# Every fourth weight tile split by the DMA: a casting load for the high part, a negation and an accumulating load for the low part

## The chip, the cores and the metric

The kernel runs on one core of one Trainium2 chip. The metric is the device time of one execution in microseconds (us). A core has a matrix engine (PE; its weight loads are listed apart as PEld), a vector engine (DVE), a scalar engine (ACT), a general-purpose engine (POOL), a queue engine that here only issues loads and stores (SP), and 16 DMA engines that all queues share.

## The reference

One layer of a streaming encoder over 256 frames of 2048 features, all in float32:

```python
xn = rmsnorm(h, norm_mix_w)
q, k, v, r, glr, gu, gv, gates = split(xn @ w_in)        # w_in: 2048 x 14352
o_gla = gla_branch(q, k, v, glr, r, ...)                 # gated linear attention
o_gmlp = gmlp_branch(gu, gv, ...)                        # spatial gating in blocks of 128 frames
g = sigmoid(gates + b_gate)
h = h + sum_b(g[b] * (branch[b] @ w_branch[b])) @ w_out  # 2 x 2048 x 2048, 2048 x 2048
hn = rmsnorm(h, norm_mlp_w)
h = h + square(relu(hn @ w_ff_up)) @ w_ff_down           # 2048 x 8192, 8192 x 2048
y = rmsnorm(h, norm_final_w)
```

Nearly all of the arithmetic is the six weight products; about 306 MB of weights are read once.

## The kernel before

**Precision.** PE multiplies in a reduced float32 format (`F32R`). To keep float32 accuracy every operand is held as two such tiles, a high part (the value rounded to `F32R`) and a low part (the value minus its high part). A product is three matmuls: high by high (L197), low activation by high weight (L198) and high activation by low weight (L199).

**Tiling.** `gemm` (L185) makes 256 tokens by 512 output columns from 2048 features. It goes over the features in 8 steps; each step needs one weight tile of 256 rows by 512 columns (512 KB; on chip 128 partitions by 1024 elements) and runs 2 feature blocks x 2 token tiles x 3 = 12 matmuls on it. A whole execution has 576 weight tiles. The matmuls of all products stand in one fixed order on PE.

**Preparing a weight tile.** `split_weights` (L170 to L183) does it in three steps on three engines. SP loads the tile into a buffer `w` (L178). ACT copies it into `wh`, which rounds it: the high part (L179). DVE subtracts `wh` from `w` into `wl`: the low part (L180). There are 5 buffers for `w` and 4 each for `wh` and `wl`, given out in turn. So the tile numbered i uses the `wh` and `wl` buffers of tile i-4, and its high part can be written only when the last matmul that reads the high part of tile i-4 (an L198) is done.

**What sets the order.** A scheduler arranges the instructions of ACT, DVE, POOL and the queues by its own estimate; each engine then runs its list in order, and waits on semaphores. During the first product (`in_order`) ACT and DVE keep the written order. Short steps (transposes, attention, norms) wait in `pending` and are worked off between weight tiles by `drain`.

**POOL** issues no DMA before. It has some memsets and, in `rsqrt_of` (L306), 20 small powers of one or two columns for the norms. ACT also moves finished products out of PSUM (`scaled`, L326), for example.

Of the kernel before, what the change touches and what calls it, by code (L numbers as in the profile page):

```python
# [9 lines left out]
F32 = mybir.dt.float32  # L10
# [32 lines left out]
class Operand:  # L43
    """An activation with features on partitions, as high and low parts: tiles of 4 K-tiles."""

# [10 lines left out]
def block_kernel(  # L56
# [21 lines left out]
    nc = tc.nc  # L78
# [18 lines left out]
    def pair_tile():  # L97
        """[128, 2, 512]: 512 features of both token tiles, tokens on partitions"""
        return slots.tile([P, NTT, CB], F32, tag="slot", name=uid("pair"))
# [18 lines left out]

    # As long as `in_order` is set, the steps on the way to the products keep their order.
    in_order = [True]  # L120

    def pin(ins):
        return tc.keep_in_program_order(ins) if in_order[0] else ins

    # Steps that need TensorE for a short time wait here, and run between the K-tiles of the
    # next large product, when what they read is long there.
    pending = deque()
# [4 lines left out]

    # ---- x, in blocks of 256 features; constants
    h = cpool.tile([P, NTT, D], F32, name="h")
# [6 lines left out]
    def late(dst, src):  # L141
        """A load that must not run ahead of the weights'."""
        tc.keep_in_program_order(nc.scalar.dma_start(dst, src))
# [15 lines left out]
    def to_partitions(src, n, name):  # L159
        """[n, 128] -> [128, n]"""  # L160
        dst = cpool.tile([P, n], F32, name=name)
        tp = tr_ps()
        nc.tensor.transpose(tp[:, 0:n], src, ident[0:n, 0:n])
        pin(nc.vector.tensor_copy(dst, tp[:, 0:n]))
        return lambda i: dst[:, i : i + 1]

    mix_col = to_partitions(vec_n, KT, "mixw")

    # ---- shared steps
    def split_weights(src, by_k=False):  # L170
        """[128, nk, n] of DRAM -> its high and low parts in SBUF."""
        k, n = src.shape[1], src.shape[1] * src.shape[2]
        w = wpool.tile([P, 2 * 528], F32, tag="w", name=uid("w"), bufs=5)
        hi = wpool.tile([P, 2 * 528], F32R, tag="wh", name=uid("wh"), bufs=4)
        lo = wpool.tile([P, 2 * 528], F32R, tag="wl", name=uid("wl"), bufs=4)
        wv, hv, lv = [t[:, 0:n].rearrange("p (k n) -> p k n", k=k) for t in (w, hi, lo)]
        for s in [slice(i, i + 1) for i in range(k)] if by_k else [slice(0, k)]:
            nc.sync.dma_start(wv[:, s], src[:, s])  # L178
            pin(nc.scalar.copy(hv[:, s], wv[:, s]))  # L179
            pin(nc.vector.tensor_tensor(  # L180
                lv[:, s], wv[:, s], hv[:, s].bitcast(F32), op=ALU.subtract
            ))
        return hv, lv  # L183

    def gemm(a, w, c0, n=CB, parts=1, k0=0, after=None, split_tail=False):  # L185
        """256 tokens of a @ w[k0 : k0 + 2048, c0 : c0 + n]: PSUM tiles [part][token tile]."""
        ps = [[mm_ps() for _ in range(NTT)] for _ in range(parts)]
# [38 lines left out]
    def to_operand_pair(dst, src, scale=None):  # L226
        """Two K-tiles of dst from src[token tile] [128, 256], tokens on partitions."""
        kt0 = dst.ready
# [28 lines left out]
    def to_operand(dst, src, scale=None):  # L257
        """to_operand_pair of four K-tiles; TensorE's way is the shorter one."""
        for half in range(2):
            part = [src[:, tt, cols(half, 2 * P)] for tt in range(NTT)]  # L260
            pending.append(lambda part=part: to_operand_pair(dst, part, scale))

    def transpose_quadrants(dst, src, jm):
        """Rows 32 jm ... of dst [128, 4 K-tiles, 256 tokens], the transpose of a pair."""
        sv = src.rearrange("p t (k m b) -> p m k t b", m=4, b=32)
        dv = dst.rearrange("p k (t i b) -> p i k t b", t=NTT, b=32)
        for i in range(4):
            nc.vector.transpose(dv[cols(jm, 32), i], sv[cols(i, 32), jm])  # L268

    def to_operand_vector(dst, src, scale=None):  # L270
        """to_operand with VectorE's transposes, in blocks of 32."""
        tr = []
# [28 lines left out]
    def rsqrt_of(sums, n, width=1):  # L301
        """(sums / n + eps) ** -0.5"""
        m = col(2)[:, 0:width]
        nc.vector.tensor_scalar(m, sums, 1.0 / n, EPS, op0=ALU.mult, op1=ALU.add)  # L304
        r = col(2)[:, 0:width]
        nc.gpsimd.tensor_tensor(r, m, mhalf[:, 0:width], op=ALU.pow)  # L306
        return r
# [14 lines left out]
    def scaled(ps, scale, func=AF.Copy):  # L322
        """func(ps * scale) of both token tiles, in SBUF."""
        res = pair_tile()
        for tt in range(NTT):
            nc.scalar.activation(res[:, tt, :], ps[tt], func, scale=scale[tt])  # L326
        return res

    # ---- the projection's operand; the rows' scale is applied behind the products
    wi = w_in[0]  # L330
# [16 lines left out]
    def transposed(ps, scale, into):  # L347
        """[256, 512] of the projection, with features on partitions."""
        sb = scaled(ps, scale)
# [20 lines left out]

    # ---- constants that are needed later
    vec_m = cpool.tile([NVEC, P], F32, name="vec_m")
# [3 lines left out]
    late(vec_m[V_BS : V_BS + GROUPS, :], b_spatial[0])  # L376
    # w_alpha_up's rows as high, low and high parts, against the gate's high, high and low parts
    wal_in = flat(slot())[0 : 3 * RANK, :]
# [40 lines left out]

    # ---- mixer A: gated linear attention  # L420
    transposed(gemm(xT, wi, C_K + CB)[0], rstd, kT)
    for i in range(2):
        pending.append(lambda i=i: wal_step(i))

    # the last head's r and the gate's low-rank rows, in one product of two parts
    ps = gemm(xT, wi, C_R + 3 * CB, n=CB + RANK, parts=2)
# [26 lines left out]

    # decays: features on partitions, tokens along the row
    E, decay, zs = [], [], []
# [16 lines left out]

    # log sigmoid(z) = min(z, 0) - ln(1 + exp(-|z|)), and its sums along each chunk
    logs = []

    def log_step(b, func, **args):
        """One function for both halves in a row: a table of functions takes long to load."""
        if func is AF.Abs:
# [44 lines left out]

    # scores[s, t] = sum_d q[t, d] k[s, d] exp(L[end of t's chunk, d] - L[s, d]), s on partitions
    S, scaled_qk = [], []
# [106 lines left out]

    # ---- gated merge of the branches
    mixed = []
# [24 lines left out]

    # ---- mixer B: gMLP spatial gating, a block of 128 frames per token tile  # L660
    ln = flat(slot())
# [57 lines left out]

    # ---- the residual, and the MLP's operand  # L720
    hT = Operand()
# [10 lines left out]

    # ---- MLP, in four stages of 2048 hidden features; the down product follows one stage behind
    def up(st, j, f):
# [26 lines left out]

    # ---- the final norm
    rest = []
# [76 lines left out]
```

## Time and profile before

| What | Value |
|---|---|
| Two runs shown | 1648.37 and 1647.96 us, median 1648.16 us |
| Profiled execution, first to last instruction (its own time; nothing else is listed for it) | 1647.4 us |
| Mean granted TensorE clock | 0.998 |
| PE busy | 1630.6 us (99%) |
| DVE busy, ACT busy, POOL busy | 1130.2 us (69%), 753.4 us (46%), 23.3 us (1%) |
| DMA | 311.75 MB, mean 189 GB/s |

The profile is one execution on the hardware profiler. Busy time is the time in which an engine had an instruction running; matmuls overlap in the pipeline, so that the spacing of their starts and not their listed duration is what one of them costs. The granted clock is 1.00 at 2.4 GHz and 0.50 at 1.2 GHz.

### The profile page before, as it was taken

What the parts mean: (1) busy time and instruction counts of PE and PEld (TensorE: products, weight loads), DVE (VectorE), ACT (ScalarE), POOL (GpSimd) and SP (SyncE); (2) the same over time, 40 slices, a digit from 0 to 9 for tenths busy, and PEclk for the clock granted to TensorE, in tenths of its full rate; (3) what the DMA queues carried; (4) which work ended last, traced back from release to release, by engine and by line L of the source; (5) the groups of instructions that cost most, each with busy time, mean ns of one, the idle gap of its engine ahead of it and who ended that gap; (6) DMA issues with size and microseconds to landing.
All of it is one profiled execution on the core that took longest, in us unless ns stands there. A gap on an engine that the chain in (4) does not pass through costs nothing.

```text
span 1647.4 us, 19352 instructions
## 1 busy us (share of the span) xinstructions
PE 1630.6 (99%) x7224; PEld 1332.3 (81%) x7224; DVE 1130.2 (69%) x1486; ACT 753.4 (46%) x864; POOL 23.3 (1%) x50
## 2 busy tenths in 40 slices
PE   8999999999999999999999999999999999999997
PEld 6878888888888888888888888888888888888886
DVE  5759576854555778877758778866666666666654
ACT  6475444544344444544445444444444444444443
POOL 0000000000000000000000000000000000000000
PEclk9999999999999999999999999999999999999999
DMA  7656566566676666666655656656556666656653
GB/s 242 205 164 179 153 181 188 179 207 197 198 209 182 190 181 185 186 204 197 196 184 185 195 169 194 207 190 188 183 182 192 193 196 199 192 190 189 214 191 114
DMA packets 163095, 311.75 MB, mean 189 GB/s; under 512 B 9812, under 2 KB 13192, under 8 KB 163000
## 3 DMA queue, kind: packets, MB, share of 16 engines
q1 hardware_dynamic: 160016, 306.35, 60.7%
q10 hardware_dynamic: 2984, 4.16, 0.8%
q8 instruction: 56, 0.92, 0.2%
q14 instruction: 39, 0.32, 0.1%
HBM read 308.37 MB, written 2.10 MB: 188 GB/s over the span
## 4 chain that ended last, share of the span: by engine, by line
PE 98%; DVE 1%; DMA 0%; issue 0%; ACT 0%; SPq 0%; POOL 0%; ACTq 0%; POOLq 0%; DVEq 0%
PE mm L199 32%; PE mm L197 32%; PE mm L198 32%; PE tr L561 1%; PE tr L609 0%; DVE slot L268 0%; PE tr L704 0%; PE tr L236 0%; DMA h<-in_x_dram 0%; DVE wl L180 0%; PE tr L464 0%; POOL col L306 0%; ACT wh L179 0%; SPq L178 0%; PE tr L412 0%
## 5 line engine op out<-in xcount | busy, mean ns | idle before, releaser
L180 DVE TENSOR_TENSOR wl<-w,wh 128x1024 fp32r<-128x1024 f32 (+2 forms) x577 | 700.8, 1222 | 450.5 <-ACT wh L179 445.6
L179 ACT CAST wh<-w 128x1024 fp32r<-128x1024 f32 (+2 forms) x577 | 602.7, 1046 | 763.0 <-PE mm L198 698.0
L199 PE MATMUL mm<-wl,slot 128*128 128x512 f32 (+1 forms) x2336 | 911.8, 390 | 1.7 <-DVE wl L180 1.7
L197 PE MATMUL mm<-wh,slot 128*128 128x512 f32 (+1 forms) x2336 | 913.3, 391 | 0.0
L198 PE MATMUL mm<-wh,slot 128*128 128x512 f32 (+1 forms) x2336 | 910.8, 390 | 0.0
L199 PEld LDWEIGHTS mm<-wl,slot 128*128 128x128 f32 x2336 | 439.0, 188 | 99.6 <-DVE wl L180 3.5
L198 PEld LDWEIGHTS mm<-wh,slot 128*128 128x128 f32 x2336 | 439.5, 188 | 96.0
L197 PEld LDWEIGHTS mm<-wh,slot 128*128 128x128 f32 x2336 | 439.6, 188 | 95.8
L268 DVE STREAM_TRANSPOSE slot<-pair 32x256 f32<-32x256 f32 x496 | 216.3, 436 | 8.3
L326 ACT ACTIVATE pair<-mm,rstd 128x512 f32<-128x512 f32 x58 | 39.8, 688 | 33.2 <-PE mm L199 33.0
L285 ACT CAST slot<-slot 128x1024 fp32r<-128x1024 f32 x23 | 24.3, 1055 | 28.3 <-DVE slot L268 28.3
L306 POOL TENSOR_TENSOR col<-col,mhalf 128x1 f32<-128x1 f32 (+1 forms) x20 | 17.9, 896 | 871.9 <-DVE col L304 579.6
L286 DVE TENSOR_TENSOR slot<-slot,slot 128x1024 fp32r<-128x1024 f32 x23 | 28.0, 1219 | 0.0
L752 DVE TENSOR_TENSOR h<-mm,h 128x512 f32<-128x512 f32 x32 | 22.1, 691 | 5.8 <-PE mm L199 5.5
L268 DVE STREAM_TRANSPOSE slot<-h 32x256 f32<-32x256 f32 x48 | 20.9, 436 | 0.9
L737 DVE TENSOR_TENSOR pair<-pair 128x1024 f32<-128x1024 f32 x16 | 19.5, 1218 | 0.0
L290 ACT ACTIVATE slot<-slot,vec 128x256 fp32r<-128x256 f32 x28 | 12.1, 499 | 15.3 <-DVE slot L268 15.3
L312 ACT ACTIVATE ev<-h 128x512 f32<-128x512 f32 x24 | 15.0, 628 | 8.1 <-DVE h L752 8.1
L251 DVE SCALAR_TENSOR_TENSOR slot<-tr,mixw,slot 128x256 fp32r<-128x256 f32 x16 | 7.0, 479 | 11.8 <-ACT slot L246 11.8
L707 DVE SCALAR_TENSOR_TENSOR pair<-tr,vec,pair 128x256 f32<-128x256 f32 x16 | 7.0, 479 | 7.5 <-PE tr L704 7.5
L291 DVE SCALAR_TENSOR_TENSOR slot<-slot,vec,slot 128x256 fp32r<-128x256 f32 x28 | 11.7, 478 | 0.0
L644 DVE SCALAR_TENSOR_TENSOR pair<-mm,rstd,bg 128x512 f32<-128x512 f32 x16 | 11.5, 749 | 0.1
(103 smaller groups left out, 260.5 us busy)
## 6 DMA issues: line engine op xcount, KB each, us to landing
w<-in_w_in_dram SPq DMA_DIRECT2D x215, 512.0 KB, 3.8
w<-in_w_ff_up_dram SPq DMA_DIRECT2D x128, 512.0 KB, 3.8
w<-in_w_ff_down_dram SPq DMA_DIRECT2D x128, 512.0 KB, 3.8
w<-in_w_branch_dram SPq DMA_DIRECT2D x64, 512.0 KB, 4.0
w<-in_w_out_dram SPq DMA_DIRECT2D x32, 512.0 KB, 4.0
w<-in_w_in_dram SPq DMA_DIRECT2D x8, 528.0 KB, 4.5
h<-in_x_dram SPq DMA_DIRECT2D x8, 256.0 KB, 7.4
bg<-in_b_gate_dram ACTq DMA_DIRECT2D x8, 256.0 KB, 4.7
```

Of the source, the lines that this page charges most:

```text
L179: pin(nc.scalar.copy(hv[:, s], wv[:, s]))
L180: pin(nc.vector.tensor_tensor(lv[:, s], wv[:, s], hv[:, s].bitcast(F32), op=ALU.subtract))
L197: pin(nc.tensor.matmul(o, lhsT=ah, rhs=wh, start=kt == 0, stop=False))
L198: pin(nc.tensor.matmul(o, lhsT=al, rhs=wh, start=False, stop=False))
L199: pin(nc.tensor.matmul(o, lhsT=ah, rhs=wl, start=False, stop=kt == KT - 1))
L268: nc.vector.transpose(dv[cols(jm, 32), i], sv[cols(i, 32), jm])
L285: nc.scalar.copy(hi, tr[0])
L286: nc.vector.tensor_tensor(lo, tr[0], hi.bitcast(F32), op=ALU.subtract)
L306: nc.gpsimd.tensor_tensor(r, m, mhalf[:, 0:width], op=ALU.pow)
L326: nc.scalar.activation(res[:, tt, :], ps[tt], func, scale=scale[tt])
L737: nc.vector.tensor_tensor(a, a, a, op=ALU.mult)
L752: nc.vector.tensor_tensor(part, ps[tt], part, op=ALU.add)
```

## The change

From the 20th call of the splitting loop on, every fourth weight tile is prepared in another way: 140 of the 576 tiles, the third and the seventh of each product. Such a tile is called a DMA tile below. Its high part comes straight from DRAM by a load issued from POOL whose destination is `F32R`, so that the DMA does the rounding. ACT then writes the negated high part into `wl` (instead of the rounding copy that it did before). A second load from POOL reads the same weights again from DRAM and adds them to what stands in `wl`, which leaves weight minus high part. SP's load and DVE's subtraction are gone for these tiles; the `w` buffer is still given out in turn but nothing writes or reads it.

```diff
+    n_split = [0]
+
     def split_weights(src, by_k=False):
...
         for s in [slice(i, i + 1) for i in range(k)] if by_k else [slice(0, k)]:
+            n_split[0] += 1
+            if n_split[0] > 16 and n_split[0] % 4 == 0:
+
+
+                nc.gpsimd.dma_start(hv[:, s], src[:, s])
+                pin(nc.scalar.activation(lv[:, s], hv[:, s].bitcast(F32), AF.Copy, scale=-1.0))
+                nc.gpsimd.dma_start(lv[:, s], src[:, s], accum_op=ALU.add)
+                continue
             nc.sync.dma_start(wv[:, s], src[:, s])
             pin(nc.scalar.copy(hv[:, s], wv[:, s]))
             pin(nc.vector.tensor_tensor(
```

The rest of the difference takes out comments, which moves line numbers: the two new loads are L184 and L186, the negation L185, the old steps L188 to L190, and the three matmuls L207 to L209.

How the order of instructions moves is shown in one product of the MLP, around two DMA tiles that follow each other (names that end in 9670 to 9672 and in 9742 to 9744). First ACT's list before the change, one rounding copy for each tile:

```order
L179 CAST wh_9653<-w_9652 128x1024
L179 CAST wh_9671<-w_9670 128x1024
L179 CAST wh_9689<-w_9688 128x1024
L179 CAST wh_9707<-w_9706 128x1024
L179 CAST wh_9725<-w_9724 128x1024
L179 CAST wh_9743<-w_9742 128x1024
L179 CAST wh_9761<-w_9760 128x1024
```

The same stretch of ACT's list now:

```order
L189 CAST wh_9653<-w_9652 128x1024
L189 CAST wh_9689<-w_9688 128x1024
L185 ACTIVATE wl_9672<-wh_9671 128x1024
L189 CAST wh_9707<-w_9706 128x1024
L189 CAST wh_9725<-w_9724 128x1024
L189 CAST wh_9761<-w_9760 128x1024
L185 ACTIVATE wl_9744<-wh_9743 128x1024
```

Each DMA tile's copy has become the negation, and it stands one place later: behind the copy of the tile after it (so at 134 of the 140; at the other 6 it stands before that copy).

POOL's list in the same stretch, with the semaphores that each instruction waits for; before the change POOL has nothing at all here:

```order
L184 DMA wh_9671<-in_w_ff_up_dram 128x2x512 [waits DMASW6_49,PE_49]
L186 DMA wl_9672<-in_w_ff_up_dram 128x2x512 [waits DMASW7_49,PE_49,Activation_49]
L184 DMA wh_9743<-in_w_ff_up_dram 128x2x512 [waits DMASW0_49,PE_49]
L186 DMA wl_9744<-in_w_ff_up_dram 128x2x512 [waits DMASW1_49,PE_49,Activation_49]
```

The casting load of a DMA tile waits for PE (the buffer's last reader), and the accumulating load waits for ACT (the negation). PE's list keeps its order; what its matmuls on a DMA tile wait for is now the DMA. The first three of the 12 on that tile:

```order
L207 MATMUL mm_9632<-wh_9671,slot_7090 128x512 [waits DMASW0_49]
L208 MATMUL mm_9632<-wh_9671,slot_7091 128x512
L209 MATMUL mm_9632<-wl_9672,slot_7090 128x512 [waits DMASW1_49]
```

The first matmul waits for the casting load, the third for the accumulating load; before, they waited for ACT's copy and for DVE's subtraction.

## Rows read from the trace of the kernel before

**Rows 1.** The page: busy time, share of the span and instructions of each engine.
```profile
PE 1630.6 (99%) x7224; PEld 1332.3 (81%) x7224; DVE 1130.2 (69%) x1486; ACT 753.4 (46%) x864; POOL 23.3 (1%) x50
```

**Rows 2.** The page: the chain that ended last, share of the span by engine.
```profile
PE 98%; DVE 1%; DMA 0%; issue 0%; ACT 0%; SPq 0%; POOL 0%; ACTq 0%; POOLq 0%; DVEq 0%
```

**Rows 3.** Groups by line: shapes, count | busy us, mean ns | idle before, and releaser.
```profile
L199 PE MATMUL mm<-wl,slot 128*128 128x512 f32 (+1 forms) x2336 | 911.8, 390 | 1.7 <-DVE wl L180 1.7
L180 DVE TENSOR_TENSOR wl<-w,wh 128x1024 fp32r<-128x1024 f32 (+2 forms) x577 | 700.8, 1222 | 450.5 <-ACT wh L179 445.6
L199 PEld LDWEIGHTS mm<-wl,slot 128*128 128x128 f32 x2336 | 439.0, 188 | 99.6 <-DVE wl L180 3.5
L306 POOL TENSOR_TENSOR col<-col,mhalf 128x1 f32<-128x1 f32 (+1 forms) x20 | 17.9, 896 | 871.9 <-DVE col L304 579.6 <-DVE col L317 292.3
```

**Rows 4.** Waits: engine, line, waited for: us in total, times, longest us.
```profile
ACT wh L179 <- PE mm L198: 698.0, 430, 2.5
```

**Rows 5.** Timeline from 801.5 us: start, us, engine, line, operation.
```profile
801.59 0.40 PE L198 MATMUL mm<-wh,slot 128*128 128x512 f32 x1
...
801.83 0.39 PE L199 MATMUL mm<-wl,slot 128*128 128x512 f32 x1
...
802.03 1.05 ACT L179 CAST wh<-w 128x1024 fp32r<-128x1024 f32 x1 [1.74 <-PE mm L198]
802.06 0.39 PE L197 MATMUL mm<-wh,slot 128*128 128x512 f32 x1
...
802.52 0.39 PE L199 MATMUL mm<-wl,slot 128*128 128x512 f32 x1
...
804.77 1.05 ACT L179 CAST wh<-w 128x1024 fp32r<-128x1024 f32 x1 [1.69 <-PE mm L198]
...
807.55 1.05 ACT L179 CAST wh<-w 128x1024 fp32r<-128x1024 f32 x1 [1.74 <-PE mm L198]
```

**Rows 6.** The tile w: all of its loads, from issue to landing.
```profile
DMA to landing us min/median/max: 3.4/3.8/8.2
```

**Rows 7.** The page: DMA queues: packets, MB, share of 16 engines.
```profile
q1 hardware_dynamic: 160016, 306.35, 60.7%
```

**Rows 8.** Timeline near the start of the program: PE's matmuls, start and us.
```profile
8.46 0.78 PE L197 MATMUL mm<-wh,slot 128*128 128x512 f32 x1
...
10.31 0.63 PE L198 MATMUL mm<-wh,slot 128*128 128x512 f32 x1
...
10.74 0.63 PE L199 MATMUL mm<-wl,slot 128*128 128x512 f32 x1
...
13.30 0.45 PE L199 MATMUL mm<-wl,slot 128*128 128x512 f32 x1
...
14.72 0.39 PE L197 MATMUL mm<-wh,slot 128*128 128x512 f32 x1
...
14.95 0.40 PE L198 MATMUL mm<-wh,slot 128*128 128x512 f32 x1
```

**Rows 9.** Timeline of PE at its longest pause, and at its end.
```profile
45.66 0.40 PE L198 MATMUL mm<-wh,slot 128*128 128x512 f32 x1
47.50 0.73 PE L199 MATMUL mm<-wl,slot 128*128 128x512 f32 x2 [1.45 <-DVE wl L180]
...
1638.24 0.40 PE L199 MATMUL mm<-wl,slot 128*128 128x512 f32 x1
```

**Rows 10.** Windows: us, busy us of PE, PEld, DVE, ACT, POOL, granted clock, DMA share, GB/s.
```profile
48.00:50.00 2.00, 2.00 (x10) 1.60 (x10) 2.00 (x3) 0.57 (x1) 0.00 (x0) 1.00 0.62 158
...
1640.00:1641.00 1.00, 0.00 (x0) 0.00 (x0) 0.21 (x1) 0.18 (x2) 0.43 (x1) 1.00 1.04 324
1641.00:1642.00 1.00, 0.00 (x0) 0.00 (x0) 0.85 (x2) 0.85 (x2) 0.12 (x1) 0.78 0.29 107
1642.00:1643.00 1.00, 0.00 (x0) 0.00 (x0) 0.30 (x1) 0.48 (x1) 0.00 (x0) 0.50 0.52 201
```

## The prediction

> **What bounds the kernel now.** I read the page's busy line first: PE is busy for 1630.6 of 1647.4 us, no other engine above 69% [rows 1]. The chain that ended last says the same, 98% of it is PE [rows 2]. Then the groups by line: PE's matmuls and weight loads waited 1.7 and 3.5 us in all for a low part from DVE [rows 3]. So the work on weight tiles is hidden, and an edit that only takes work off DVE or SP can gain next to nothing: at most these 5.2 us, 0.3%, while about 2% is what a measurement of this kernel can tell from no change.
>
> The question is therefore how much room the hidden work has. The waits show that ACT's copy of a tile mostly waits for PE to leave the buffer (430 times, 698.0 us) [rows 4], so the buffers, not the loads, set its start. The timeline shows the rhythm [rows 5]: the last reader of a high part starts at 801.59 and ends at 801.99, ACT's copy into that buffer starts at 802.03, and PE starts the next tile at 802.06. The copies start at 802.03, 804.77 and 807.55, so a tile takes (807.55 - 802.03) / 2 = 2.76 us. The buffer freed at 801.99 belongs to a tile that PE begins three tiles later, at 802.06 + 3 x 2.76 = 810.34. Its high part is needed then, its low part at the third matmul, 0.46 us later (802.52 against 802.06). So from the freeing of a buffer there are 8.35 us until the high part and 8.81 us until the low part is needed. I call the second number the cover. Before, copy (1.05) and subtraction (1.22) need 2.3 us of it, because the load runs ahead into the five buffers of `w`.
>
> **The change, part by part.**
>
> Removed: 140 subtractions on DVE (140 x 1.222 = 171 us), 140 loads from SP and 140 copies on ACT. All lie beside PE's matmuls, so they count as nothing. ACT gets 140 negations of the copies' shape in return; I price one like a copy, 1.05 us.
>
> Added, and on the path: the load of a DMA tile no longer runs ahead. It writes into `wh` itself, so it can start only when PE has left the buffer of tile i-4. With 4 buffers and every fourth tile, the DMA tiles always use the same buffer, one after the other. After the freeing come, in a row: the casting load, the negation, the accumulating load. None can overlap, since each reads what the one before wrote. Their sum, the chain, stands against the cover.
>
> - Casting load. No load from POOL and no cast by DMA is in the trace. The nearest row is SP's load of the same 512 KB: 3.4 to 8.2 us, median 3.8 [rows 6]. Below, 3.4; I see no reason for less. POOL must write the transfer's descriptors by an instruction of its own; its small powers take 0.9 us on average [rows 3], and I add one such: 3.8 + 0.9 = 4.7. Above, 8.2 + 0.9 = 9.1.
> - Negation: 1.05, plus nothing for its place behind the next tile's copy. That copy may start one tile after the freeing and ends at 2.76 + 1.05 = 3.8 us, before the 4.7 at which the casting load lands. If the load came at 3.4, the negation would start 0.4 late.
> - Accumulating load. Besides the weights it must read the old content of `wl`. The weight loads held the 16 DMA engines for 60.7% of 1647.4 us, 1000 us for 306.35 MB / 0.524 = 584 tile loads' worth, 1.71 us each [rows 7]. I add one more such pass for the second operand: 3.8 + 0.9 + 1.7 = 6.4. Below, 3.4 (the second read costs nothing); above, 9.1 + 1.7 = 10.8, or more if the addition itself is slow, for which no row gives a bound.
> - Hops between engines: PE to ACT takes 0.04 us [rows 5]; for four of them, with one through POOL's queue, 0.2.
>
> Chain: 4.7 + 1.05 + 6.4 + 0.2 = 12.35 us, between 8.05 and 21.2. Against the cover PE waits 12.35 - 8.81 = 3.5 us at the third matmul of each DMA tile. The loads for the high part alone would be covered (4.7 against 8.35). 140 x 3.5 = 490 us.
>
> The clock comes on top. At 2.4 GHz matmuls start 0.23 us apart, near the program's start 0.43 us apart, the lower of the two levels (10.31 to 10.74, against 14.72 to 14.95) [rows 8]; the clock column reads 1.00 there too, so I go by the spacing. PE's longest pause in the middle, from 46.06 to 47.50, left the clock at 1.00. At the end the last matmul ended at 1638.64, and the granted clock fell to 0.50 (1.2 GHz) between 1641 and 1642, by the window's mean of 0.78 at 1641.56, after 2.9 us of idle [rows 9, 10]. A stall of 3.5 us is longer than that. Near the start the slow spacing lasts from 8.46 to about 13.3 [rows 8], over 10 matmuls. After a stall, the 10 matmuls left on the DMA tile would then run at 0.43 instead of 0.23, 2.0 us more. They stand before the freeing of the buffer from which the next chain starts, so they lengthen the period in full: 140 x 2.0 = 280 us.
>
> The Trainium skill bears on this (TensorE: Matmul & The Clock Gate, section HAM oscillation — how this bites in real kernels): a kernel whose bursts of matmuls wait for a DMA between them can lose the clock in every round. This trace has one fall and one pause without it, and no repeated stall. By the rule the sum is 1648 + 490 + 280; if the clock held it would be 1648 + 490.
>
> Hidden, with its cover: the copy of tile i+2 stands behind the negation on ACT. The negation ends 5.8 us after the freeing, the copy at 6.9, its subtraction at 8.1; PE needs it at 5 x 2.76 = 13.8. That room stays as long as the casting load lands within some 10 us. PSUM evacuations on ACT have a whole product of slack. On POOL, 8 of the 20 small powers now stand between a tile's two loads, and others behind the accumulating load and its wait; at most one tile of 2.76 us each, 9 x 2.76 = 25 us with the one memset that lies there, and I take 0.
>
> The DMA engines: in four tiles three plain loads, the casting load and the accumulating one take 3 x 1.71 + 1.71 + 3.42 = 10.3 us of a period that grows to some 16.6 us. They do not bound.
>
> Sum: against the profiled execution's 1647.4 us (0.8 below the median of 1648.16, so I add to the median): 1648 + 490 + 280 = 2418, rounded to 2420 us.
>
> **The rivals.**
>
> *The stall without the fall of the clock.* If the chain is under 8.81 + 2.9 = 11.7 us, or if the clock stands a pause of 3.5 us, only the stall counts. With both loads at 4.7 the chain is 10.65, the stall 1.84, the time 1648 + 258 = 1906; with 12.35 it is 2138. For it: the pause at 46 us went by without a fall. Against it: the fall at the end after 2.9 us.
>
> *The chain fits into the cover.* If loads from POOL land like SP's fastest, the chain is 3.4 + 0.4 + 1.05 + 3.4 + 0.2 = 8.45 us, below 8.81: PE never waits, and the time is 1648 less at most 5, the same as before. The point of decision is two loads of 3.6 us on average. Against it: half of SP's own loads take 3.8 or more, and the second reads two operands. The Trainium skill gives a fit for a load from POOL (DMA: Bandwidth & Descriptors, section Anatomy of one DMA — SWDGE (gpsimd) path): 2.0 us plus the bytes at 436 GB/s, 3.2 us for 512 KB by my estimate. By that page the chain would be 7.65 or, with the negation held behind its neighbour, some 8.3, and nothing would be lost; no run here shows it.
>
> *The accumulating load is slow.* If the addition runs at a fraction of the copy's rate, that load becomes the period. At 10.8 us, with the casting load at 5.5, the chain is 17.55, the stall 8.7, and the time 1648 + 140 x (8.7 + 2.0) = 3146. Nothing in the trace speaks for or against it.
>
> That the change doesn't do what it says can be left out: the lists of instructions hold the 280 loads on POOL with the waits named above. A gain over 2% would need 33 us and only 5.2 us of waits are there.
>
> **How the numbers follow.** Forecast, stall and fall of the clock with chains of 11.7 to 16 us: 0.48. Stall alone: 0.29. Slow accumulation: 0.14. Chain in the cover: 0.08. A gain: 0.01. The point is the forecast's 2420. The low end, 1900, is the stall with both loads at 4.7; the high end, 2950, is a chain of 16.1 us with the clock's fall (1648 + 140 x 9.3), which leaves out most of the slow accumulation and the case of no change. Slower by over 2% (above 1681) takes the three cases with a stall, less 0.01 for a stall under 0.24 us: 0.90. Within 2%: 0.09. Faster: 0.01.
>
> **What would show it.** Right: idle time of PE before the third matmul of a DMA tile (L209), released by the DMA into `wl`, 140 times and some 3.5 us each; nothing before the first matmul (L207); POOL's casting loads at 4 to 5.5 us and its accumulating loads at 6 to 8 us from issue to landing; DVE's busy time down by 171 us; the granted clock's mean well below 1, with 0.43 us spacing behind the stalls. Wrong: PE still 98% busy (the chain is covered); idle before L207 (the casting load alone overruns its 8.35 us); idle released by ACT or DVE (their lists, not the DMA, are late); idle before L209 with the clock at 1.00 throughout.

## The result, and the profile after

The changed kernel takes 2473.91 us (2467.67 to 2480.16, two runs) against 1648.16 us: a ratio of 1.5006, 95% interval 1.4976 to 1.5037. It is 826 us slower, 5.9 us for each of the 140 DMA tiles.

The page of the changed kernel: busy time by engine, the chain that ended last by engine, and the two large DMA queues (packets, MB, share of the 16 engines). They answer to [rows 1, 2, 7].

```profile
span 2478.4 us, 19347 instructions
...
PE 1912.3 (77%) x7224; PEld 1499.6 (61%) x7224; DVE 967.2 (39%) x1346; ACT 742.7 (30%) x864; POOL 294.2 (12%) x330
...
q0 software_dynamic: 76160, 146.88, 29.5%
q1 hardware_dynamic: 121936, 232.91, 29.1%
...
DMA 41%; issue 28%; PE 25%; POOL 3%; ACT 1%; DVE 1%; POOLq 0%; SPq 0%; ACTq 0%; DVEq 0%
```

The chain has gone over from PE (98%) to the DMA (41%); the 28% called issue are mostly POOL's time from one casting load to the accumulating load behind it, that is, the casting load and the negation. Two things add up to the loss. PE idles for 2478.4 - 1912.3 = 566.1 us instead of 16.8, which is 549 more; and it is busy for 1912.3 - 1630.6 = 282 us more with the same 7224 matmuls. Together that is 831 us, the difference of the two spans.

The groups by line (after the bar: busy us, mean ns | idle before, and its releasers), to be held against [rows 3]:

```profile
L209 PE MATMUL mm<-wl,slot 128*128 128x512 f32 (+1 forms) x2336 | 1031.2, 442 | 550.5 <-DMA wl<-in_w_in_dram 178.2 <-DMA wl<-in_w_ff_down_dram 141.1 <-DMA wl<-in_w_ff_up_dram 125.4
L207 PE MATMUL mm<-wh,slot 128*128 128x512 f32 (+1 forms) x2336 | 1003.5, 430 | 0.0
...
L190 DVE TENSOR_TENSOR wl<-w,wh 128x1024 fp32r<-128x1024 f32 (+2 forms) x437 | 533.1, 1222 | 956.8 <-ACT wh L189 953.7
...
L185 ACT ACTIVATE wl<-wh 128x1024 fp32r<-128x1024 f32 (+1 forms) x140 | 148.2, 1059 | 39.4 <-DMA wh<-in_w_in_dram 21.7 <-DMA wh<-in_w_ff_down_dram 7.3 <-DMA wh<-in_w_ff_up_dram 6.7
```

All of the new idle time stands before one matmul, the first that reads a low part, and the loads into `wl` end it. That PE's list keeps its order, as said above, holds for 98 of the 140 DMA tiles: in 41 others this matmul stands fourth or fifth instead of third. The first matmul of a tile (L207) waits for nothing: the casting load is in time.

The landing times of all loads into `wh` and into `wl`, from issue, for [rows 6]; the first line is the casting load, the second the accumulating one:

```profile
DMA to landing us min/median/max: 3.8/4.0/6.6
...
DMA to landing us min/median/max: 5.6/7.5/11.9
```

One round in the MLP, as the timeline shows it (start, us, engine, line):

```profile
1506.46 0.63 PE L208 MATMUL mm<-wh,slot 128*128 128x512 f32 x1
...
1507.39 0.74 POOL L184 DMA_DIRECT2D wh<-in_w_ff_up_dram  x1 [9.00 <-PE mm L208]
...
1510.95 1.05 ACT L189 CAST wh<-w 128x1024 fp32r<-128x1024 f32 x1 [10.16 <-PE mm L208]
...
1511.90 1.06 ACT L185 ACTIVATE wl<-wh 128x1024 fp32r<-128x1024 f32 x1
...
1513.26 1.20 POOL L186 DMA_DIRECT2D wl<-in_w_ff_up_dram  x1 [5.13 <-ACT wl L185]
...
1516.78 0.40 PE L208 MATMUL mm<-wh,slot 128*128 128x512 f32 x1
1521.03 0.79 PE L209 MATMUL mm<-wl,slot 128*128 128x512 f32 x1 [3.86 <-DMA wl<-in_w_ff_up_dram]
```

The buffer is free at 1507.09, POOL issues the casting load 0.30 us later, the negation runs from 1511.90, the accumulating load is issued at 1513.26, and PE goes on at 1521.03: 13.9 us. Over the 137 rounds whose stall the timeline names, the mean is 0.30 to POOL, 4.45 to the negation, 1.06 for it, 0.34 to POOL, 7.50 to the matmul, 13.66 us in all. Of the 4.45 us the load itself takes 4.12 on average, and for the remainder the negation stands behind other work on ACT: 83 of the 140 negations start directly behind another instruction. In the round shown the casting load has landed at 1511.52, but the copy of the next tile, which waited for the slow PE, runs until 1512.00. Before, PE waited for no load of weights: there the load ran ahead into `w`.

The windows around that stall (from and to in us, their length, then busy us of PE, PEld, DVE, ACT, POOL, granted clock, DMA share, GB/s):

```profile
1516.00:1518.00 2.00, 1.18 (x6) 0.60 (x4) 0.65 (x2) 1.05 (x1) 0.00 (x0) 1.00 0.85 173
...
1519.00:1520.00 1.00, 0.00 (x0) 0.00 (x0) 0.00 (x0) 0.00 (x0) 0.00 (x0) 0.74 1.09 236
1520.00:1521.00 1.00, 0.00 (x0) 0.00 (x0) 0.00 (x0) 0.00 (x0) 0.00 (x0) 0.50 1.01 348
...
1524.00:1526.00 2.00, 2.00 (x6) 1.52 (x6) 0.00 (x0) 0.00 (x0) 0.46 (x1) 0.50 0.00 0
1526.00:1528.00 2.00, 2.00 (x10) 1.60 (x9) 0.00 (x0) 0.00 (x0) 0.28 (x1) 0.92 0.51 129
```

PE's last matmul ends at 1517.18, and the clock falls to 0.50 (1.2 GHz) at about 1519.5, in the middle of the stall. The matmuls after it run six in 2 us instead of ten, until the clock is back at 2.4 GHz shortly after 1526. It does not always fall inside a stall: of the 127 falls before the program's end 65 come while PE stands, and 62 after PE has gone on, 0.8 us later on average. The mean granted clock of the whole run is 0.878.

### The profile page after: what moved, and what is told of

Its sections match the earlier page's. It is cut to its first block, busy times and chain, and to the rows that moved or that the text cites. A ratio compares the mean times of both kernels' runs of the same rounds, so it can differ in the third digit from the quotient of the medians.

```text
span 2478.4 us, 19347 instructions
## 1 busy us (share of the span) xinstructions
PE 1912.3 (77%) x7224; PEld 1499.6 (61%) x7224; DVE 967.2 (39%) x1346; ACT 742.7 (30%) x864; POOL 294.2 (12%) x330
## 4 chain that ended last, share of the span: by engine, by line
DMA 41%; issue 28%; PE 25%; POOL 3%; ACT 1%; DVE 1%; POOLq 0%; SPq 0%; ACTq 0%; DVEq 0%
DMA wl<-in_w_in_dram 14%; PE mm L209 11%; DMA wl<-in_w_ff_down_dram 10%; DMA wl<-in_w_ff_up_dram 9%; PE mm L208 7%; PE mm L207 7%; DMA wl<-in_w_branch_dram 5%; POOL wh L184 3%; DMA wl<-in_w_out_dram 3%; ACT wl L185 1%; PE tr L571 0%; DMA wh<-in_w_ff_up_dram 0%; DVE slot L278 0%; DVE wl L190 0%; ACT wh L189 0%
## 5 line engine op out<-in xcount | busy, mean ns | idle before, releaser
L209 PE MATMUL mm<-wl,slot 128*128 128x512 f32 (+1 forms) x2336 | 1031.2, 442 | 550.5 <-DMA wl<-in_w_in_dram 178.2
L207 PE MATMUL mm<-wh,slot 128*128 128x512 f32 (+1 forms) x2336 | 1003.5, 430 | 0.0
L208 PE MATMUL mm<-wh,slot 128*128 128x512 f32 (+1 forms) x2336 | 1000.2, 428 | 0.0
L209 PEld LDWEIGHTS mm<-wl,slot 128*128 128x128 f32 x2336 | 500.0, 215 | 723.4 <-DMA wl<-in_w_in_dram 199.6
L190 DVE TENSOR_TENSOR wl<-w,wh 128x1024 fp32r<-128x1024 f32 (+2 forms) x437 | 533.1, 1222 | 956.8 <-ACT wh L189 953.7
L189 ACT CAST wh<-w 128x1024 fp32r<-128x1024 f32 (+2 forms) x437 | 455.6, 1045 | 1228.7 <-PE mm L208 1140.7
L208 PEld LDWEIGHTS mm<-wh,slot 128*128 128x128 f32 x2336 | 497.3, 213 | 117.1
L207 PEld LDWEIGHTS mm<-wh,slot 128*128 128x128 f32 x2336 | 499.4, 214 | 112.9 <-ACT pair L336 0.2
L185 ACT ACTIVATE wl<-wh 128x1024 fp32r<-128x1024 f32 (+1 forms) x140 | 148.2, 1059 | 39.4 <-DMA wh<-in_w_in_dram 21.7
L184 POOL DMA_DIRECT2D wh<-in_w_in_dram x52 | 38.7, 744 | 487.4 <-PE mm L208 283.4
L186 POOL DMA_DIRECT2D wl<-in_w_in_dram x52 | 62.7, 1206 | 239.3 <-ACT wl L185 239.3
L184 POOL DMA_DIRECT2D wh<-in_w_ff_down_dram x32 | 23.6, 739 | 337.1 <-PE mm L208 230.2
L184 POOL DMA_DIRECT2D wh<-in_w_ff_up_dram x32 | 23.7, 739 | 325.2 <-PE mm L208 222.3
L186 POOL DMA_DIRECT2D wl<-in_w_ff_down_dram x32 | 38.4, 1201 | 166.9 <-ACT wl L185 166.9
L186 POOL DMA_DIRECT2D wl<-in_w_ff_up_dram x32 | 38.5, 1202 | 155.3 <-ACT wl L185 155.3
L184 POOL DMA_DIRECT2D wh<-in_w_branch_dram x16 | 11.8, 739 | 160.7 <-PE mm L208 112.7
```

The source lines that it names most:

```text
L184: nc.gpsimd.dma_start(hv[:, s], src[:, s])
L185: pin(nc.scalar.activation(lv[:, s], hv[:, s].bitcast(F32), AF.Copy, scale=-1.0))
L186: nc.gpsimd.dma_start(lv[:, s], src[:, s], accum_op=ALU.add)
L190: pin(nc.vector.tensor_tensor(lv[:, s], wv[:, s], hv[:, s].bitcast(F32), op=ALU.subtract))
L207: pin(nc.tensor.matmul(o, lhsT=ah, rhs=wh, start=kt == 0, stop=False))
L208: pin(nc.tensor.matmul(o, lhsT=al, rhs=wh, start=False, stop=False))
```

## The experiments

Theory: after a buffer is freed, three steps follow one another (casting load, negation, accumulating load), and their sum is longer than the 8.81 us until the low part is needed; the fall of the clock adds to it. The main rivals: the additional bytes, the accumulating load by itself, and the clock as a loss with its full 282 us.

**Own buffers for the DMA tiles.** A DMA tile's chain may now start one DMA tile earlier.

```diff
+        own = not by_k and n_split[0] + 1 > 16 and (n_split[0] + 1) % 4 == 0
+        tag, bufs = ("s", 2) if own else ("", 3)
+        hi = wpool.tile([P, 2 * 528], F32R, tag="wh" + tag, name=uid("wh"), bufs=bufs)
+        lo = wpool.tile([P, 2 * 528], F32R, tag="wl" + tag, name=uid("wl"), bufs=bufs)
+        w = hi if own else wpool.tile([P, 2 * 528], F32, tag="w", name=uid("w"), bufs=3)
```

> The DMA tiles get two high and two low buffers of their own, the other tiles three of each, and the unused w buffers go (3 of w, for the other tiles alone). All 280 loads from POOL and their bytes stay. Theory (chain longer than the cover): a DMA tile's chain, 13.66 us on average in the changed kernel, now starts when the DMA tile eight places earlier is done, about 8.8 + 4 x 2.76 = 19.9 us ahead, so PE no longer waits: 1648 us (1640 to 1660), clock near 1.00, no idle before the third matmul of a DMA tile. Rival (the extra bytes or the addition load the 16 DMA engines, so that waiting cannot be hidden): above 2200 us, with idle before the low part still some 500 us.

Measured: 1724.8 us, ratio 1.0481 (1.0432 to 1.0530), clock 0.994 in the profiled execution (1740.9 us). All 280 loads are still there, and 749 of the 826 us are gone: the missing head start, not the work, made the loss. But 76 us stay, which the theory did not expect. The waits of this kernel show who stands now (engine, line, waited for: us in total, times, longest):

```profile
POOL wl L188 <- ACT wl L187: 1278.0, 139, 14.6
DVE wl L192 <- ACT wh L191: 694.6, 189, 10.2
ACT wl L187 <- DMA wh<-in_w_ff_down_dram: 222.1, 32, 10.3
ACT wl L187 <- DMA wh<-in_w_in_dram: 199.8, 45, 9.6
```

ACT now waits at the negation for the casting load, whose median landing has grown from 4.0 to 9.2 us, and the copies of plain tiles queue behind it. POOL's timeline in the MLP shows that this load is issued 0.73 us behind the accumulating load of the DMA tile before:

```profile
1304.04 1.20 POOL L188 DMA_DIRECT2D wl<-in_w_ff_up_dram  x1 [11.37 <-ACT wl L187]
1304.77 1.22 POOL L186 DMA_DIRECT2D wh<-in_w_ff_up_dram  x1
```

**Five buffers for all tiles.** One more tile of cover, nothing else (`bufs=5` for `wh` and `wl`, 3 for `w`, which DMA tiles no longer take).

> Five instead of four buffers for the high and the low parts of all tiles (and 3 of w, not given out for DMA tiles). Theory: the cover grows by one tile to 8.81 + 2.76 = 11.57 us, the chain stays 13.66, the stall is 2.1 us, too short for the clock to fall: 1648 + 140 x 2.1 = 1942 us (1880 to 2000), granted clock at least 0.98. Rival (the clock falls at any repeated stall): 2050 us or more with a clock of 0.93 or less. Rival (DMA load, not the buffers, sets the time): 2350 us or more.

Measured: 1903.02 us, ratio 1.154 (1.149 to 1.159), clock 0.983. The time is the theory's, to 39 us: one more buffer took away 571 us, 4.1 us a tile. The remaining stalls are 1.56 us on average (115 of them, 179.5 us), 370 us less in sum; the other part is the clock, which falls 16 times instead of 127, so that PE is busy for 1690.8 us instead of 1912.3. The two terms of the expectation are both off, though, and largely cancel: casting loads land after 5.8 instead of 4.1 us on average, which makes the chain 15.0 and not 13.66 us, and from the freeing of the buffer to the stop of PE there are 13.8 instead of 9.7 us, 4.0 more and not 2.76. The buffer is now freed one tile earlier, before the DMA tile in between, so the stall of that tile counts as cover too.

**The clock held up.** Matmuls that nobody reads fill the wait.

```diff
                 pin(nc.tensor.matmul(o, lhsT=al, rhs=wh, start=False, stop=False))
+                if fill[0]:
+                    fill[0] = False
+                    junk = tr_ps()
+                    for _ in range(FILL):
+                        pin(nc.tensor.matmul(junk[:, 0:m], lhsT=ah, rhs=wh, start=True, stop=True))
```

> 16 matmuls into a spare PSUM tile, read by nobody, stand in PE's list before the third matmul of each DMA tile, where PE waits; all else is the changed kernel. They keep PE busy for 16 x 0.23 = 3.7 us of the wait. Theory: the clock stays at 1.00 and the wait for the low part stays; the 10 matmuls between the low part's arrival and the freeing of the buffer take 2.3 us instead of the 3.6 measured, so the time falls by 140 x 1.3 = 180 us to 2290 (2240 to 2340). Rival (the fall of the clock costs its whole extra busy time of PE, 282 us): 2190 us. Rival (the fall costs nothing because PE waits anyway): 2474 us with the clock at 1.00.

Measured: 2348.08 us, ratio 1.424 (1.421 to 1.427), clock 0.989. 126 us come back, less than the 180 of the expectation and 8 us outside its band; of the rivals, both the 282 and the nothing are out. The accumulating load is still what PE waits for: it lands 7.55 us after its issue on average (7.42 in the changed kernel). From the end of the wait to the next casting load there are 2.82 instead of 3.89 us: 1.07 x 140 = 150 us. A mean round is 0.97 us shorter (16.24 against 17.21), 136 us; in about a dozen tiles the added matmuls outlast the load. PE's list differs a little too (139 DMA tiles have the low part third, 98 in the changed kernel), so the clock is not quite the only difference.

**The casting load alone.** The negation and the accumulating load go, DVE's subtraction is back.

```diff
                 nc.gpsimd.dma_start(hv[:, s], src[:, s])
-                pin(nc.scalar.activation(lv[:, s], hv[:, s].bitcast(F32), AF.Copy, scale=-1.0))
-                nc.gpsimd.dma_start(lv[:, s], src[:, s], accum_op=ALU.add)
+                nc.sync.dma_start(wv[:, s], src[:, s])
+                pin(nc.vector.tensor_tensor(
+                    lv[:, s], wv[:, s], hv[:, s].bitcast(F32), op=ALU.subtract
+                ))
```

> Of the change only the casting load is left: the high part of a DMA tile by the load from POOL, the weights also by SP's load, the low part by DVE's subtraction as before. The bytes read stay those of the changed kernel. Theory: freeing to high part 0.3 + 4.5 us, subtraction 1.2, some 6.1 us in all, inside the cover of 8.8: 1648 us (1640 to 1665). Rival (a casting load from POOL that waits for its buffer is already too late, or the doubled reading costs): idle before the first matmul of DMA tiles and over 1700 us.

Measured: 1762.16 us, ratio 1.0694 (1.0676 to 1.0712). A miss: I expected no loss, and found 114 us. The time is the rival's, its sign hardly: the named waits of PE are at DVE's subtractions (42.0 us), and only 8.7 us stand at a first matmul for the casting load. In this run casting loads land after 6.2 us (3.9 to 9.5), probably because more plain loads go on beside them, which no run separates; on average that is still 2.3 us before the tile's first matmul. DVE's list stands at the subtraction until then (403 us in the largest four waits of that line), and with it everything behind it on DVE.

**The accumulating load alone.** SP's load and ACT's copy are back for the high part, the rest stays.

> Of the change only the negation and the accumulating load are left: the high part of a DMA tile by SP's load and ACT's copy as before, then the negation, then the accumulating load; buffers as in the changed kernel. Theory (the steps after the freeing add up): 0.04 + 1.05 + 1.06 + 0.34 + 7.5 = 10.0 us against the cover of 8.81, a stall of 1.2 us: 1648 + 140 x 1.2 = 1816 us (1770 to 1880), clock at least 0.98. Rival (the accumulating load alone makes the loss): still above 2300 us. Rival (only both loads together make it, this one alone hides): 1648 us.

Measured: 1856.06 us, ratio 1.126 (1.124 to 1.128), clock 0.981. Inside the theory's band: without the 4.75 us of the casting load in front, the same 7.6 us of the accumulating load cost 208 us instead of 826. Both parts alone make 114 + 208 = 322 us; the other 504 us come only when they stand in one chain.

**Without the addition.** The second load overwrites (`accum_op` left out).

> The second load from POOL writes the weights over the negated high part instead of adding them, so the low parts of the DMA tiles hold the rounded weights and not the remainder; all waits, bytes read from DRAM and orders stay. Theory (the addition reads a second operand and holds the DMA engines for 3.4 instead of 1.8 us): this load lands in 4.2 to 5 us instead of 7.5, the chain is 10.4 to 11.2 us, the stall 1.6 to 2.4: 1870 to 1985 us, clock 0.97 or more. Rival (the 7.5 us are the waiting of any second load from POOL, not the addition): 2474 us.

Measured: 2048.95 us, ratio 1.243 (1.240 to 1.247), clock 0.951. The landing times of loads into `wl` in this kernel:

```profile
DMA to landing us min/median/max: 3.9/5.0/8.6
```

So the addition is 2.5 of the 7.5 us, and leaving it out gives back 425 of the 826 us. POOL's instruction is 0.72 us here instead of 1.20. The time is 64 us over the band: the load and the stalls (2.05 us on average, 275 in sum) are as I thought, but the clock fell more often (0.951 instead of 0.97), and PE is busy for 1755.5 us, 125 more than before the change.

**The load issued ahead.** For what own buffers left over, I suspected a ring on POOL's list; here the next casting load is issued before this accumulating load.

```diff
+            hv = ahead.pop(num)
+            load_high(num + 4)
             lo = wpool.tile([P, 2 * 528], F32R, tag="wls", name=uid("wl"), bufs=2)
             lv = lo[:, 0:n].rearrange("p (k n) -> p k n", k=k)
             pin(nc.scalar.activation(lv, hv.bitcast(F32), AF.Copy, scale=-1.0))
-            nc.gpsimd.dma_start(lv, src, accum_op=ALU.add)
+            tc.keep_in_program_order(nc.gpsimd.dma_start(lv, src, accum_op=ALU.add))
```

> As e1_own_buffers, but POOL issues the casting load of the next DMA tile before the accumulating load of this one (three high buffers for DMA tiles; one buffer less for short-lived vectors). Theory on what e1_own_buffers left over (76 us): a ring on POOL and ACT, in which the next casting load stands behind this accumulating load, which waits for the negation, which waits for the casting load: 9.1 + 1.06 + 0.33 + 1.82 = 12.3 us a round against 11.4 us for four tiles at full speed. With the load ahead the ring is gone: 1648 us (1640 to 1675). Rival (the bytes: the DMA engines are 82% busy there, and plain loads land late): 1710 to 1740 us again, with idle of PE behind copies and subtractions of plain tiles.

Measured: 1726.89 us, ratio 1.0477 (1.0459 to 1.0494). A miss in the time, which is that of own buffers again. But the same time is lost in other places. All kernels run the weight products in the same order on PE, so the start of the same matmul can be compared (us; the kernel before, then how much later the others are in their profiled executions; the last column is the next experiment):

| Matmul | before | own buffers | load ahead | none in gating |
|---|---|---|---|---|
| first of the gating stage | 480.4 | 21.9 | 17.3 | 18.0 |
| first of the third product behind that stage | 708.1 | 36.1 | 68.4 | 30.6 |
| first of the second MLP product | 953.2 | 50.1 | 77.0 | 39.2 |
| last of all products | 1638.2 | 91.5 | 77.7 | 40.0 |

In the MLP, from its second product on, own buffers lose 41 us bit by bit and the load ahead loses 0.7 us. There the theory of the ring held: what the ring cost is gone. (This version also has three high buffers for DMA tiles instead of two; which of the two did it is not separated.) What it loses instead comes in steps. Four of 12.4 to 13.3 us each stand in and just behind the gating stage. The first of them, on POOL and on PE:

```profile
545.96 0.73 POOL L361 TENSOR_TENSOR col<-col,mhalf 128x2 f32<-128x2 f32 x1 [25.26 <-DVE col L359]
550.41 2.20 POOL L361 TENSOR_TENSOR col<-col,mhalf 128x2 f32<-128x2 f32 x1 [3.72 <-DVE col L359]
552.57 0.75 POOL L210 DMA_DIRECT2D wh<-in_w_in_dram  x1
553.32 1.27 POOL L225 DMA_DIRECT2D wl<-in_w_in_dram  x1
554.06 1.28 POOL L210 DMA_DIRECT2D wh<-in_w_in_dram  x1
...
561.14 1.22 PE L254 MATMUL mm<-wl,slot 128*128 128x512 f32 x2 [7.80 <-DMA wl<-in_w_in_dram]
```

Three loads leave POOL in a row, right behind a power for which POOL had waited 25 us and another for which it had waited 3.7 us, and PE then stands for 7.80 us at a low part. All four are alike (us in total, times, longest):

```profile
PE mm L254 <- DMA wl<-in_w_in_dram: 32.8, 4, 8.6
```

**No DMA tiles in the gating stage.** Same kernel, the 16 DMA tiles of that stage prepared like the others (`by_dma(num)` leaves out the products 20 to 27).

> As e7_load_ahead, but the 16 DMA tiles of the eight products in the spatial gating stage are prepared like the others (124 DMA tiles are left). In that stage e7_load_ahead lost 46 us of its 78 (397 against 351 us from the first load of w_spatial to the first of w_out), and there POOL's list has the powers of the norms, which wait some 25 us for DVE, in front of both loads of a DMA tile. Theory (these powers hold the loads back): 1727 - 46 = 1681 us (1665 to 1695), the stage as long as before. Rival (the stage loses for another reason, its copies and transposes on ACT and DVE): 1710 to 1730 us.

Measured: 1689.99 us, ratio 1.0254 (1.0237 to 1.0271). Inside the theory's band. From the first load of `w_spatial` to the first of `w_out` it takes 357.8 us instead of 397.2 (before 350.8). Three of the four steps are gone, 38.5 us by the table's matmuls. The fourth stays: it stands in the first product behind the stage, whose DMA tiles are still there, and costs 12.6 us. Leaving out the DMA tiles takes work off ACT and DVE too, so this run alone does not decide for the powers; that the steps stand right behind them in POOL's list does. The 40 us that are left are 18.0 up to the stage, this step, 8.4 in the first product of the MLP, right behind two powers as well, and 1 us in all other places.

**The accumulating load alone, with own buffers.**

> As e3_accum_only, with own buffers for the DMA tiles (two high, two low; three of each and three of w for the rest). The weights of a DMA tile are still read twice, once by SP, once by the accumulating load. Theory: POOL has one load for a DMA tile and no ring, the chain of 10.0 us starts about 19.9 us ahead: 1648 us (1640 to 1675). Rival (bytes and DMA engines' share): 1700 us or more, as in e1_own_buffers and e2_cast_only.

Measured: 1766.82 us, ratio 1.071 (1.068 to 1.074). Own buffers took 89 of the 208 us of the accumulating load, and no more; PE still waits for loads into `wl`. The theory of a head start of 19.9 us fails here, and the trace says where:

```profile
SPq L186 <- DVE wl L193: 531.4, 131, 9.9
...
ACT wh L187 <- DMA w<-in_w_in_dram: 58.6, 33, 4.0
```

SP's load for a DMA tile (L186) waits 131 of 140 times for a subtraction on DVE, which frees a `w` buffer: this version has three of them for all tiles, where the changed kernel has five. The copy into `wh` (L187) then waits for that load in 111 of 140 cases (33 of them in the line shown), when its own high buffer has been free for 10.8 us (median). So the chain starts with the load into `w`, 15.7 us (median) ahead of the low part, and that buffer, not the own ones, sets its head start. A version with five `w` buffers was not run.

**The bytes alone.** The kernel before, with 280 loads more that nobody waits for.

```diff
-            nc.sync.dma_start(wv[:, s], src[:, s])
+            n_split[0] += 1
+            tc.keep_in_program_order(nc.sync.dma_start(wv[:, s], src[:, s]))
+            if n_split[0] > 16 and n_split[0] % 2 == 0:
+                tc.keep_in_program_order(nc.sync.dma_start(scratch, src[:, :, 0:CB]))
```

> The kernel before, with 280 more loads of 512 KB (every second weight tile once more, from SP, into a tile that nobody reads; one buffer less for short-lived vectors): as many bytes from DRAM beside the weights as the changed kernel's 280 loads from POOL, and with 280 x 1.71 = 479 us about the DMA engines' time of e7_load_ahead, a share of some 90%. Theory (what the runs with own buffers, with the casting load alone and with the accumulating load alone lose against before comes from lists on POOL, ACT and DVE that stand still until a load from POOL lands, not from the bytes): 1648 us (1640 to 1665), since plain loads have several tiles of slack. Rival (the bytes alone delay the plain loads and PE with them): 1690 us or more, with idle of PE behind copies and subtractions of plain tiles.

Measured: 1648.47 us, ratio 1.0001 (0.9991 to 1.0010). Its page:

```profile
PE 1630.5 (99%) x7224; PEld 1331.3 (81%) x7224; DVE 1130.4 (69%) x1486; ACT 753.4 (46%) x864; POOL 23.3 (1%) x50
...
DMA packets 239257, 458.58 MB, mean 279 GB/s; under 512 B 14292, under 2 KB 17672, under 8 KB 239160
...
q1 hardware_dynamic: 236176, 453.17, 83.9%
```

The DMA engines are 84% busy with plain loads and PE loses nothing. So the additional bytes, read by plain loads, are not the cause of these losses by themselves. That a load from POOL lands later in other versions (4.0 us in the changed kernel, 6.2 and 9.2 us where PE hardly stalled) matters because lists stand still for it. The same unread traffic as casting or accumulating loads from POOL was not tried.

None of these versions is faster than the kernel before, nor can one be by much: PE is the bound there.

## Why the prediction was right

- *The bound and the small gain.* Right: DVE's 140 subtractions went (1130.2 to 967.2 us busy), and nothing was gained by it.
- *The chain against the cover.* Right in its mechanism and place. The buffers decide: one more took 571 us, own ones 749 us. Predicted were 12.35 us, measured 13.66, on average over all DMA tiles: casting load 4.7 and 4.12; negation 1.05 and 1.06, and its place in ACT's list, put at nothing, 0.33; accumulating load 6.4 and 7.42; hops 0.2 and 0.7 (0.32 to POOL, 0.34 from ACT to POOL, the remainder to PE). That freeing to negation came out as predicted (4.75 us) is luck: the load was shorter, the hop and ACT's list were longer.
- *The term that was too small* is the accumulating load, by 1.0 us on average. One more pass of the DMA engines was right as their time: queue q0's share is 0.295 x 2478.4 = 731 us for 140 pairs, 5.2 us a pair; the casting load alone held the engines for 14.5% of 1756.5 us, 1.82 us a load, and the accumulating load alone for 25.6% of 1853.0 us, 3.39 us a load (predicted 3.42). But the landing grew by more than this pass. Without the addition the load lands after 5.0 us, 0.3 over my 4.7; with it 2.5 us later, 0.8 over my 1.7. POOL's instruction is listed 0.48 us longer with the addition (1.20 against 0.72 us), which may be part of this; the rest is open.
- *The stall.* Predicted 490 us (3.5 us a tile), measured 549 (3.9). Less than the longer chain would make, because the slow matmuls behind a stall lengthen the cover: from the freeing to the stop of PE there are 9.7 us in the changed kernel, and with the clock held up 12.8, which is 9.1 without the 3.7 us of added matmuls.
- *The clock.* That it falls came as predicted, nearly once a round (after 2.3 us of idle in the one shown). PE's busy time grew by 282 us, predicted 280. But the step "They stand before the freeing of the buffer from which the next chain starts, so they lengthen the period in full" was wrong: held up, the clock gives back 126 us. Only part of the slow matmuls stand before the freeing (in the round shown the buffer is free at 1507.09, and the slow spacing goes on in the next tile); those behind it shorten the wait that follows.
- *The sum.* 2420 against 2474 us, 2% short, is in part luck. With the clock held up the loss was still 700 us, where the prediction's stall alone made 490 (2138 us): 210 too little. The fall of the clock cost 126 us and not 280: 154 too much. The two errors nearly cancel. The terms were right as shares of the trace (490 and 280 against 549 and 282), and not as what each would save if it were gone.
- *The rival of the chain that fits.* The Trainium skill's fit for a load from POOL gives 3.2 us for 512 KB, by estimate (DMA: Bandwidth & Descriptors, section Anatomy of one DMA — SWDGE (gpsimd) path). Measured from issue to landing: 4.0 us for the casting load, 7.5 us for the accumulating one, of which 2.5 us are the addition. The measurement decides: no pair of loads here is short enough.
- *What I had put at nothing* for POOL's powers was nothing in the changed kernel: no casting load left POOL later than 1 us after its buffer was free. It is not nothing once the chain is covered: with the load ahead, the steps behind powers in and after the gating stage and at the start of the MLP make some 59 of the 78 us. Lists of ACT and DVE that stand at a load cost more in the other versions.

## What to carry to other kernels

When a transfer moves from a buffer of its own into the buffer that the consumer reads, it loses its head start: count the steps between the freeing of that buffer and its next use, and hold their sum of latencies, not their throughput, against the time that the number of buffers gives. A wait for a DMA on an engine's in-order list stops everything behind it there, so look at what else that list carries. Two costs read from one trace (a stall and a slow clock behind it) need not add up as savings. Two versions with the same time can lose it in different places: compare when the same instruction starts, before a theory is given up.

## What the runs showed of the hardware that was not expected

- POOL starts a load 0.30 us after its releaser, where ACT starts 0.04 us after PE [rows 5]; in the changed kernel its instruction is listed with 0.74 us for the casting and 1.20 us for the accumulating load of 512 KB (0.72 without the addition; 1.22 for casting loads issued right behind an accumulating one).
- An accumulating load holds the DMA engines twice as long as a casting one (3.39 against 1.82 us, each alone), and the latter hardly longer than a plain one (1.71 us).
- 84% busy DMA engines did no harm to plain loads that run ahead by several tiles; the casting load of 512 KB from POOL landed in 4.0 us in the changed kernel, in 6.0 with the load ahead and in 9.2 us right behind an accumulating load (medians).
